# Four moves in one decoder block: a sum of squares two pumps later, two inverses on another DMA queue, a recurrence one pump later, a last norm one pump sooner

## The chip, the core and the metric

The kernel runs on one core of a Trainium2 chip. A core has five engines that work side by side, each with its own instruction stream: TensorE (PE in the profile; PEld is its weight load), VectorE (DVE), ScalarE (ACT), GpSimd (POOL) and SyncE (SP), which here only issues DMAs. DMAs can be issued from the streams of SP, ACT and GpSimd; an issue stands in order with that engine's other work. The metric is the time of one execution on the device in microseconds (us); lower is better. Several runs of the kernel are given with their median, and one more execution was recorded by the profiler.

## The reference

One decoder block on x of 512 tokens by 2048, in fp32. An adaLN vector c gives shifts, scales and gates; two token mixers run side by side on the normed input; a SwiGLU channel mixer follows, and a last RMSNorm.

```python
mod = c_act @ w_ada[l] + b_ada[l]
sh_a, sc_a, gt_a, sh_f, sc_f, gt_f = ...
h = _rmsnorm(x, norm_mix[l]) * (1.0 + sc_a) + sh_a
p = h @ w_in[l]
c_q, c_kv, k_pe, q_g, k_g, v_g, z, b_logit, a_logit, gate_logits = _split_cols(p)
y_a = _mla_branch(c_q, c_kv, k_pe, ...) @ w_o_mla[l]
y_b = _gdn_branch(qkv, z, b_logit, a_logit, ...) @ w_o_gdn[l]
g_a, g_b = jnp.split(jax.nn.sigmoid(gate_logits), 2, axis=-1)
x = x + gt_a * ((g_a * y_a + g_b * y_b) @ w_o[l])
h = _rmsnorm(x, norm_ffn[l]) * (1.0 + sc_f) + sh_f
gate, up = jnp.split(h @ w_gate_up[l], 2, axis=-1)
x = x + gt_f * ((jax.nn.silu(gate) * up) @ w_down[l])
return _rmsnorm(x, final_norm)
```

Two parts of it matter here. The first `_rmsnorm(x, ...)` needs the sum of squares of every token over 2048 channels. The gated DeltaNet branch (`_gdn_branch`) works on 8 heads in chunks of 64 tokens, and for every chunk and head it solves with a unit lower triangular 64 by 64 matrix:

```python
Lmat = jnp.where(strict, jnp.einsum('bhncd,bhnsd->bhncs', kb, k) * decay, 0.0)
A = Lmat + jnp.eye(CHUNK)
sol = lax.linalg.triangular_solve(A, rhs, left_side=True, lower=True, unit_diagonal=True)
```

The kernel inverts these triangles instead: 32 by 32 diagonal blocks first, by forward substitution on VectorE, then the off-diagonal blocks of 32 and of 64 by small products on TensorE.

## The kernel before

**Products and weights.** An fp32 product is made of three products of halves. Each weight tile of 128 by 1024 is loaded (`raw`), rounded into `hi` on ACT (L263), and the rest goes into `lo` on VectorE (L264); activations have such halves too (`hh`, `hl`). A weight unit, two k-tiles, is 24 matmuls on TensorE: hh by hi, hl by hi, hh by lo. There are five raw slots (`RAWS`) and four pairs of hi and lo (`SPLITS`). All matmuls, and all DMAs of `load` (on SP's queue) and `side` (on GpSimd's queue), carry line 155, that of a helper; so they are told apart by their tiles.

**Chains and pumps.** The main line is a list of units. Everything else (statistics, the DeltaNet groups, norms) is written as Python generators, called chains. The driver (L49 to L127) counts the matmuls of the main line and after every 12 (`GROUP`) it "pumps": each chain runs up to its next `yield`. `yield n` lets n pumps go by. So a number behind a `yield` says how many times 12 matmuls stand on TensorE between two steps of a chain. Where the main line needs a result, it runs the chain to its end at once (`drv.finish`). The order on SP, GpSimd and TensorE is the program's order; that on VectorE and ACT is set by a planner when the kernel is built, with the program's data dependencies kept. All engines then run their streams in order.

**The sum of squares.** `x_statistics` (L460) adds the squares of the 16 channel tiles on VectorE (`x_sum`, L456), then TensorE sums over the partitions in eight small instructions (`xss`, four matmuls in the code), VectorE takes the reciprocal root (L396, L229 to L233) and puts it on a diagonal (`diag`, L472), and a product with ones spreads it to all partitions (`rbc`, copied to `r_all` on ACT, L476). The main line, which is then multiplying `ga` products, needs `r_all` where the fully normed input is first used: `start_h` (L1499) calls `drv.finish(chains["stat"])` there. On VectorE the sums of `rawm` run beside this: `rawm` tiles are those of w_ada, 192 loads of 512 KB on SP's queue that take the same raw slots, and each is multiplied and summed in one operation (L435).

**The DeltaNet groups.** `gdn(g)` is one chain for each of two groups of heads. Forward substitution on VectorE (L797, L799) fills `fsX`; it is written to DRAM (`fso`, two DMAs, L803) and read back in another layout (`T32`, four DMAs, L807; the profile calls it T). Fourteen pumps later come T's transpose (L815), the products `M1` (profile: M) with copies on ACT (L825) and VectorE (L826), three pumps later `X1` (profile: X) with negated copies into `T64` (L847, ACT) and `T64T` (L848, VectorE), then `M2` with copies on ACT (L867), three pumps later `X2` with negated copies (L878), and then the recurrence over chunks (`py`, `pks`, `po`). Beside it on ACT run the copies of the conv inputs (`cp`, L523) and of the conv's first tap (L510), on VectorE the other taps (`cv`, L513).

**The tail.** `finished` (L2006) is a chain that the last down-projection unit of the first half of the tokens adds: it sums squares on TensorE (`hss`), takes the reciprocal root, spreads it (`hbc`), scales x (L2013) and writes it out in eight DMAs, while the main line multiplies the last `dnt` products of the second half.

Of the kernel before, what the change touches and what calls it, by code (L numbers as in the profile page):

```python
# [171 lines left out]
def block_kernel(ctx: ExitStack, tc: tile.TileContext, a: dict, out, out_t):  # L172
    nc = Core(tc, PINNED)
# [16 lines left out]
    def S(s, dt=F32):  # L190
        return slots.tile([P, 512], dt, tag="s", name=nm(s))

    def PS(s):
        return psum.tile([P, 512], F32, tag="ps", name=nm(s))
# [4 lines left out]
    def load(dst, src):  # L199
        nc.sync.dma_start(dst, src)  # L200

    def side(dst, src):
        nc.gpsimd.dma_start(dst, src)
# [3 lines left out]
    def tok(j):  # L207
        return slice(j * P, (j + 1) * P)
# [184 lines left out]
    def token_rstd(ss, n, inv):  # L393

        v, y, u = (C(nm("rs"), [P, n]) for _ in range(3))
        nc.vector.tensor_scalar(v[:], ss, inv, EPS, op0=ALU.mult, op1=ALU.add)  # L396
        rsqrt(y[:], v[:], u[:])
        return y
# [50 lines left out]
    def square(k):  # L449

        if k == 0:
            nc.scalar.activation(x_sum[:], xT[k][:], AF.Square)
            return
        s = S("sq")
        tc.keep_in_program_order(nc.scalar.activation(s[:], xT[k][:], AF.Square))
        tc.keep_in_program_order(nc.vector.tensor_tensor(x_sum[:], x_sum[:], s[:], ALU.add))  # L456
# [3 lines left out]
    def x_statistics():  # L460
        for k in range(KT):
            square(k)
            if k % 2:
                yield
        yield 2
        ps = PS("xss")
        for t in range(NT):
            mm(ps[:, t:t + 1], x_sum[:, tok(t)], ones[:, 0:1], start=True, stop=True)
        x_rstd = token_rstd(ps[:, 0:NT], NT, 1.0 / D)
        diag = S("diag")  # L470
        for t in range(NT):
            nc.vector.tensor_scalar(diag[:, tok(t)], ident, x_rstd[:, t:t + 1], None, op0=ALU.mult)  # L472
        yield 5
        ps = PS("rbc")
        mm(ps[:], ones[:], diag[:], start=True, stop=True)
        nc.scalar.copy(r_all[:], ps[:])  # L476
# [85 lines left out]
    def head():  # L562
# [39 lines left out]
        for k in range(KT):  # L602
# [9 lines left out]
            u.post()  # L612
        drv.deep = AHEAD
        chains["stat"] = drv.add(x_statistics())

    wide = S("wide", F32R)
# [80 lines left out]
    fso = [dram.tile([4, NT, 4, 32, 32], F32, name=f"fso{g}") for g in range(2)]  # L697

    def gdn(g):
# [89 lines left out]
        fsX = fsX_[:].rearrange("p (i a) -> p i a", a=16)  # L789
# [10 lines left out]
            if j % 4 == 3:  # L800
                yield
        for hf in range(2):
            nc.scalar.dma_start(fso[g].rearrange("b c h i a -> (b c h) i a")[:, :, 16 * hf:16 * hf + 16], fsX[64 * hf:64 * hf + 64])  # L803
        del fsX_, fsX, fsT, fsL
        T32 = S("T32")
        for b in range(4):
            nc.scalar.dma_start(T32[32 * b:32 * b + 32, :].rearrange("p (n a) -> p n a", a=32),  # L807
                                fso[g][b].rearrange("c h i a -> i (c h) a"))
        yield 14
        T64 = [S("T64"), S("T64")]  # L810
# [48 lines left out]
        for hf in range(2):  # L859
# [6 lines left out]
            m2 = S("M2")  # L866
            nc.scalar.copy(m2[64:128, :], p3[64:128, :])  # L867
            M2.append(m2)
        yield 3
        for hf in range(2):  # L870
            p4 = PS("X2")
            for c in (2 * hf, 2 * hf + 1):
# [427 lines left out]
    def view(tile_, seg):  # L1300

        return tile_[:].rearrange("p (k n) -> p k n", k=2)[:, :, seg[1]:seg[1] + seg[2]]
# [11 lines left out]
    def part_rstd(segs):  # L1314

        ps = PS("hss")
        n = sum(seg[2] for seg in segs) // P
        todo = []
        for i in range(max(len(sums[seg]) for seg in segs)):
            t0 = 0  # L1320
            for seg in segs:
                if i < len(sums[seg]):
                    v = view(sums[seg][i], seg)
                    todo += [(t0 + t, v[:, j, tok(t)]) for t in range(seg[2] // P) for j in range(2)]
                t0 += seg[2] // P
        for i, (t, v) in enumerate(todo):
            mm(ps[:, t:t + 1], v, ones[:, 0:1], start=i == 0, stop=i == len(todo) - 1, skip_group_check=True)
        for seg in segs:
            del sums[seg]
        y = token_rstd(ps[:, 0:n], n, 1.0 / D)  # L1330
        diag = S("diag")
        for t in range(n):
            nc.vector.tensor_scalar(diag[:, tok(t)], ident, y[:, t:t + 1], None, op0=ALU.mult)
        return diag, n * P

    def spread(diag, n):
        ps = PS("hbc")
        mm(ps[:, 0:n], ones[:], diag[:, 0:n], start=True, stop=True)
        return ps[:, 0:n]
# [153 lines left out]
    def mixing():  # L1493
# [25 lines left out]
        def start_a():  # L1519
            ch["A"] = drv.add(gdn(0))  # L1520
# [6 lines left out]
        def start_b():  # L1527
            ch["B"] = drv.add(gdn(1))
# [316 lines left out]
    def ffn():  # L1845
# [126 lines left out]
        def last_unit(segs, fs):  # L1972
# [15 lines left out]
            def post():  # L1988
                for i, f in enumerate(fs):
                    o = 0  # L1990
                    for h, c0, m in segs:
                        add_gated(h, f, box["ps"][i][:, o:o + m], gt_ffn, c0)
                        o += m
                q = fs[0] // 2
                for seg in segs:
                    squares(q, seg, nc.gpsimd if q < 7 else nc.vector)
                for h, c0, m in segs:
                    for k in fs:
                        v = half_of(x2[h][q], k)[:, c0:c0 + m]
                        nc.scalar.activation(v, v, AF.Copy, scale=n_out[:, k:k + 1])  # L2000
                if q == 7:
                    drv.add(finished(segs))
# [1 line left out]
            return Unit(mms=mms, pre=pre, post=post)  # L2004

        def finished(segs):  # L2006
            yield 2
            diag = part_rstd(segs)
            yield 2
            r = spread(*diag)  # L2010
            for q in range(8):
                v = view(x2[0][q], segs[0])
                nc.vector.tensor_tensor(v, v, r.unsqueeze(1).broadcast_to([P, 2, 256]), ALU.mult)  # L2013
                load(out[256 * q:256 * q + 256, :].rearrange("(k p) n -> p k n", p=P), v)
                if q % 2:
                    yield
# [89 lines left out]
```

## Time and profile before

| | us |
|---|---|
| three runs | 2811.27, 2808.55, 2806.51 |
| their median | 2808.55 |
| profiled execution | 2811.78 |
| its span | 2810.0 |
| TensorE busy | 2777.4 (99% of the span) |
| VectorE busy | 1876.6 (67%) |
| ACT busy | 1040.1 (37%) |
| GpSimd busy | 175.2 (6%) |

The span runs from the first to the last instruction; 1.8 us of the profiled execution lie around it. The mean granted clock of TensorE was 0.995 of full speed. In the rows of the profile, a line such as `138.62 1.86 PE L155 MATMUL xss<-ones,x_sum ... x8 [4.97 <-DVE x_sum L456]` gives the start, the duration, the engine, the line of the kernel, the operation, output and inputs, shape and count; the bracket gives the idle time of that engine before it and what ended it. "ACTq" is the issue side of ACT, where its DMAs are issued. A windows row gives the length of a stretch, then the busy time and count of each engine, the granted clock, the busy share of the DMA engines, and GB/s.

### The profile page before, as it was taken

To read this page: it belongs to the slowest core of one execution; us is meant where nothing else is said; L and a number is where in the kernel's file an instruction comes from. 1 tells how busy PE (TensorE), PEld (TensorE's weight loads), DVE (VectorE), ACT (ScalarE), POOL (GpSimd) and SP (SyncE) were. 2 spreads that over 40 slices of the span, in tenths; PEclk is the share of its full clock that TensorE was granted. 3 is DMA by queue.
4 is the path that set the end of the run, shared out by engine and by line. 5 is a ranking of instruction groups with operands and counts; after the bars stand their busy time and mean duration, and the time that the engine had idled before them with its cause. 6 is when DMAs were issued, how large, how long until landed. Compare 5 with 4: busy or idle time off the path is not lost.

```text
span 2810.0 us, 43334 instructions
## 1 busy us (share of the span) xinstructions
PE 2777.4 (99%) x16944; PEld 2473.5 (88%) x16944; DVE 1876.6 (67%) x3172; ACT 1040.1 (37%) x1433; POOL 175.2 (6%) x250
## 2 busy tenths in 40 slices
PE   9999999999999999999999999999999999999997
PEld 7788788788888888888999999999999998888887
DVE  8884666666868547774587888888888873223235
ACT  3443432442344343222374444444444442112123
POOL 0000011001000000001000000000000040030001
PEclk9999999999999999999999999999999999999999
DMA  9995555545646549885453443344344475363241
GB/s 352 320 374 172 159 174 176 173 134 166 190 131 192 191 142 327 286 292 170 160 175 96 137 136 125 129 136 136 124 132 136 136 260 174 113 206 123 98 135 61
DMA packets 307014, 495.22 MB, mean 176 GB/s; under 512 B 47380, under 2 KB 160180, under 8 KB 306680
## 3 DMA queue, kind: packets, MB, share of 16 engines
q1 hardware_dynamic: 260232, 417.03, 45.7%
q0 software_dynamic: 14304, 46.45, 4.6%
q10 hardware_dynamic: 32272, 28.97, 3.1%
q8 instruction: 132, 2.16, 0.3%
q14 instruction: 74, 0.61, 0.1%
HBM read 440.97 MB, written 51.40 MB: 175 GB/s over the span
## 4 chain that ended last, share of the span: by engine, by line
PE 93%; DVE 3%; DMA 2%; issue 1%; ACT 1%; ACTq 0%; SPq 0%; DVEq 0%; POOL 0%; POOLq 0%
PE m L155 29%; PE dn L155 15%; PE wo L155 6%; PE gb L155 5%; PE v L155 4%; PE gu L155 3%; PE z L155 3%; PE ya L155 3%; PE yb L155 3%; PE s L155 3%; PE k L155 2%; PE ga L155 2%; PE qk L155 2%; PE ckv L155 2%; PE q L155 2%; PE cq L155 1%
## 5 line engine op out<-in xcount | busy, mean ns | idle before, releaser
L264 DVE TENSOR_TENSOR lo<-raw,hi 128x1024 fp32r<-128x1024 f32 x338 | 413.8, 1227 | 452.7 <-ACT hi L263 443.6
L263 ACT CAST hi<-raw 128x1024 fp32r<-128x1024 f32 (+1 forms) x338 | 352.4, 1044 | 938.9 <-PE dn L155 255.3
L435 DVE CUSTOM_DVE_ANT_0 rawm<-rawm,cbc 128x1024 f32<-128x1024 f32 x192 | 232.9, 1225 | 150.0 <-DMA rawm<-in_w_mod_dram 149.9
L1720 ACT CAST hi<-sums 128x1024 fp32r<-128x1024 f32 x160 | 167.8, 1049 | 325.9 <-PE m L155 234.2
L155 PE MATMUL m<-h2h,lo 128*128 128x256 f32 x960 | 271.7, 283 | 0.0
L155 PE MATMUL m<-h2l,hi 128*128 128x256 f32 x960 | 271.7, 283 | 0.0
L155 PE MATMUL m<-h2h,hi 128*128 128x256 f32 x960 | 271.7, 283 | 0.0
L1721 DVE TENSOR_TENSOR lo<-sums,hi 128x1024 fp32r<-128x1024 f32 x160 | 195.8, 1224 | 109.7 <-ACT hi L1720 109.6
L155 PE MATMUL dn<-ah,hi 128*128 128x512 f32 x640 | 249.1, 389 | 0.0
L155 PE MATMUL dn<-al,hi 128*128 128x512 f32 x640 | 249.0, 389 | 0.0
L155 PE MATMUL dn<-ah,lo 128*128 128x512 f32 x640 | 249.0, 389 | 0.0
L155 PEld LDWEIGHTS m<-h2h,hi 128*128 128x128 f32 x960 | 184.3, 192 | 0.0
L155 PEld LDWEIGHTS m<-h2l,hi 128*128 128x128 f32 x960 | 184.3, 192 | 0.0
L155 PEld LDWEIGHTS m<-h2h,lo 128*128 128x128 f32 x960 | 184.3, 192 | 0.0
L1720 ACT CAST hi<-raws 128x768 fp32r<-128x768 f32 x160 | 133.5, 834 | 118.0 <-PE m L155 88.8
L1721 DVE TENSOR_TENSOR lo<-raws,hi 128x768 fp32r<-128x768 f32 x160 | 152.1, 951 | 3.4 <-ACT hi L1720 3.4
L155 PEld LDWEIGHTS dn<-ah,hi 128*128 128x128 f32 x640 | 120.1, 188 | 25.4 <-DVE g L1737 0.3
L155 PEld LDWEIGHTS dn<-ah,lo 128*128 128x128 f32 x640 | 120.1, 188 | 24.9
L155 PEld LDWEIGHTS dn<-al,hi 128*128 128x128 f32 x640 | 120.1, 188 | 24.8
L1712 DVE TENSOR_TENSOR sums<-sums,raws 128x256 f32<-128x256 f32 x320 | 134.3, 420 | 4.2
L1712 DVE TENSOR_TENSOR sums<-raws 128x512 f32<-128x512 f32 x160 | 109.9, 687 | 8.8 <-DMA raws<-in_w_gate_up_dram 6.1
L155 PE MATMUL wo<-mh,hi 128*128 128x512 f32 (+1 forms) x320 | 111.2, 347 | 0.0
(498 smaller groups left out, 7202.3 us busy)
## 6 DMA issues: line engine op xcount, KB each, us to landing
rawm<-in_w_mod_dram SPq DMA_DIRECT2D x192, 512.0 KB, 5.4
raws<-in_w_gate_up_dram SPq DMA_DIRECT2D x320, 256.0 KB, 3.0
raw<-in_w_in_dram SPq DMA_DIRECT2D x144, 512.0 KB, 4.5
raw<-in_w_down_dram SPq DMA_DIRECT2D x88, 512.0 KB, 3.8
raw<-in_w_o_dram SPq DMA_DIRECT2D x40, 512.0 KB, 3.9
rawa<-in_w_in_dram SPq DMA_DIRECT2D x32, 512.0 KB, 4.3
raw<-in_w_gate_up_dram SPq DMA_DIRECT2D x48, 256.0 KB, 3.0
a_dram<-ah POOLq DMA_DIRECT2D x40, 256.0 KB, 2.4
```

Source lines behind the costliest of these rows:

```text
L155: return self.tc.keep_in_program_order(f(*args, **kwargs))
L263: nc.scalar.copy(hi[:], raw[:])
L264: (lo_eng or nc.vector).tensor_tensor(lo[:], raw[:], hi[:].bitcast(F32), ALU.subtract)
L435: nc.vector.tensor_tensor_reduce(raw, raw, c, 1.0, 0.0, ALU.mult, ALU.add, parts[:, k, half:half + 1])
L1712: add = lambda o, x, y: nc.vector.tensor_tensor(o, x, y, ALU.add)
L1720: nc.scalar.copy(hi[:], src)
L1721: nc.vector.tensor_tensor(lo[:], src, hi[:].bitcast(F32), ALU.subtract)
```

## The change

Four edits, in three chains and one queue:

- `x_statistics`: `yield 2` before the `xss` products becomes `yield 4`. The products stand two pumps (24 matmuls) later.
- `gdn`, L803 and L807: the DMAs that write `fso` and read `T32` are issued with `side`, on GpSimd's queue, where they were issued on ACT's. Twelve DMAs in all, six for each group, with the same sizes and layouts.
- `gdn`, L869: `yield 3` between M2 and X2 becomes `yield 4`. X2 and all that follows in the group stand one pump (12 matmuls) later.
- `finished`: the first `yield 2` becomes `yield`. The sums of squares of the last first-half segment stand one pump sooner, with what follows.

No product, copy or DMA is added or removed. The planner sets the order on VectorE and ACT anew.

```diff
@@ x_statistics
             if k % 2:
                 yield
-        yield 2
+        yield 4
         ps = PS("xss")
@@ gdn
         for hf in range(2):
-            nc.scalar.dma_start(fso[g].rearrange("b c h i a -> (b c h) i a")[:, :, 16 * hf:16 * hf + 16], fsX[64 * hf:64 * hf + 64])
+            side(fso[g].rearrange("b c h i a -> (b c h) i a")[:, :, 16 * hf:16 * hf + 16], fsX[64 * hf:64 * hf + 64])
         del fsX_, fsX, fsT, fsL
         T32 = S("T32")
         for b in range(4):
-            nc.scalar.dma_start(T32[32 * b:32 * b + 32, :].rearrange("p (n a) -> p n a", a=32),
+            side(T32[32 * b:32 * b + 32, :].rearrange("p (n a) -> p n a", a=32),
                                 fso[g][b].rearrange("c h i a -> i (c h) a"))
         yield 14
@@ gdn
             M2.append(m2)
-        yield 3
+        yield 4
         for hf in range(2):
             p4 = PS("X2")
@@ finished
         def finished(segs):
-            yield 2
+            yield
             diag = part_rstd(segs)
```

## The prediction

> **What bounds the kernel now.** I read the busy times first. TensorE has 1% of the span left, so an edit is worth what it does to TensorE's stalls, to its clock, or to the ends of the span.
>
> ```profile
> PE 2777.4 (99%) x16944; PEld 2473.5 (88%) x16944; DVE 1876.6 (67%) x3172; ACT 1040.1 (37%) x1433; POOL 175.2 (6%) x250
> ```
>
> The waits of TensorE come next. Each happened once; the third is the start of the kernel, and what is not shown is below 1 us.
>
> ```profile
> PE xss L155 <- DVE x_sum L456: 5.0, 1, 5.0
> PE k L155 <- DVE lo L264: 3.7, 1, 3.7
> PE cb L155 <- DMA crow<-in_c_dram: 3.1, 1, 3.1
> PE X L155 <- issue: 1.7, 1, 1.7
> ```
>
> The windows view shows that the other three each cost more than the wait. Its columns are length, busy time of PE, PEld, DVE, ACT and POOL, then TensorE's granted clock, the DMA share and GB/s.
>
> ```profile
> 137.55:144.38 6.83, 5.76 (x18) 4.89 (x19) 5.97 (x14) 1.58 (x2) 0.00 (x0) 0.50 0.87 293
> 144.38:153.00 8.62, 8.62 (x40) 7.12 (x39) 7.68 (x20) 2.87 (x5) 0.60 (x2) 1.00 0.92 313
> 516.43:523.26 6.83, 5.12 (x12) 4.06 (x13) 6.78 (x11) 4.29 (x9) 0.00 (x0) 0.50 0.55 172
> 560.80:567.63 6.83, 6.83 (x28) 5.65 (x29) 6.34 (x12) 1.88 (x3) 0.00 (x0) 0.50 0.31 97
> ```
>
> Around each wait lies a stretch of 6.83 us at half clock. Busy TensorE in it does half the work, so half its busy time is lost: 2.88, 2.56 and 3.41 us. With the waits, the three places cost 7.85 us (xss), 6.25 us (k) and 5.11 us (X). The four edits touch these three and the tail. [...]
>
> The unit of all shifts is the price of one matmul, from a row of the chain of waits:
>
> ```profile
> 154.24 43.53 PE ga L155 x192
> ```
>
> 43.53 / 192 = 0.227 us; a pump (12 matmuls) is 2.72 us, a unit (24) 5.44 us.
>
> **A: the xss products two pumps later (L465).** It adds and removes nothing. The eight products move behind 24 further ga matmuls; rbc does not move, because the start of the next stage forces the chain to its end there.
>
> ```profile
> 133.26 0.39 PE L155 MATMUL ga<-hh,lo 128*128 128x512 f32 x1
> 138.62 1.86 PE L155 MATMUL xss<-ones,x_sum 128*128 128x1 f32 x8 [4.97 <-DVE x_sum L456]
> 137.88 0.68 DVE L456 TENSOR_TENSOR x_sum<-x_sum,sq 128x512 f32<-128x512 f32 x1
> 140.52 0.16 DVE L396 TENSOR_SCALAR rs<-xss 128x4 f32<-128x4 f32 x1 [0.81 <-PE xss L155]
> 140.60 1.23 DVE L264 TENSOR_TENSOR lo<-raw,hi 128x1024 fp32r<-128x1024 f32 x1
> 151.90 0.92 DVE L472 TENSOR_SCALAR diag<-kc,rs 128x128 f32<-128x128 f32 x4
> 152.69 1.22 DVE L435 CUSTOM_DVE_ANT_0 rawm<-rawm,cbc 128x1024 f32<-128x1024 f32 x1
> L155 PE MATMUL rbc<-diag,ones x2: 590/590/591, 153.2 to 153.7; 128*128 128x512 f32 x2
> 138.50:152.80 14.30, 14.18 (x55) 11.85 (x56) 12.50 (x32) 3.34 (x5) 0.54 (x1) 0.79 0.91 307
> ```
>
> Today TensorE gets to xss at about 133.5 and waits for x_sum until 138.6. With 24 matmuls more it gets there at 133.5 + 5.44 = 138.9, after x_sum is done: the wait of 4.97 goes, and the half clock with it. But the next thing is late. From xss to rbc VectorE needs 14.3 us and is busy for 12.5 of them; it runs the rsqrt steps between the sums of rawm and the lo halves, in an order fixed ahead. TensorE has 24 matmuls instead of 48 between xss (about 1 us at full clock) and rbc, so it is at rbc at 138.9 + 1 + 5.4 = 145.3 and waits for diag, some 8.6 us. What counts is when rbc can run. VectorE's order changes in two places: the lo of 140.60 now stands ahead of L396 (that moves the chain by about half a microsecond, which later idle time absorbs), and the rawm sum of 152.69 (1.22 us) now stands ahead of diag. That makes diag about 1.1 us later: rbc at 154.3 instead of 153.2. After a stall this long TensorE restarts at half clock; now it is at full clock there. By the two restarts above (2.88, 2.56) I take 2.6. A = +1.1 + 2.6 = **+3.7 us**. Ends: +1.4 (diag 0.3 early, half of half a stretch, 1.7) and +4.8 (1.4 late, half of 6.83). The lo halves are too far ahead of TensorE afterwards to hide any of it elsewhere, so it goes into the end.
>
> **B: the inverses' way through DRAM on GpSimd's queue (L803, L807).** Two writes of 128 KB and four reads of 64 KB per group leave ACT's queue, where each stands in order with ACT's work.
>
> ```profile
> 496.47 3.98 ACTq L803 DMA_DIRECT2D fso<-fsX  x2
> 500.54 1.06 ACT L263 CAST hi<-raw 128x1024 fp32r<-128x1024 f32 x1 [12.88 <-DMA fso<-fsX]
> 503.68 2.50 ACTq L807 DMA_DIRECT2D T<-fso  x4
> 506.22 2.06 ACT L523 COPY cp<-q 128x512 f32<-128x512 f32 x4 [4.62 <-issue]
> 500.64 1.23 DVE L435 CUSTOM_DVE_ANT_0 rawm<-rawm,cbc 128x1024 f32<-128x1024 f32 x1 [4.25 <-DMA rawm<-in_w_mod_dram]
> 508.93 8.02 DVE L513 SCALAR_TENSOR_TENSOR cv<-cp,columns,cv 128x511 f32<-128x511 f32 x12 [5.92 <-ACT cv L510]
> 516.86 3.49 DVE L264 TENSOR_TENSOR lo<-raw,hi 128x1024 fp32r<-128x1024 f32 x3
> 518.14 0.80 PE L155 MATMUL k<-hh,lo 128*128 128x512 f32 x1 [3.69 <-DVE lo L264]
> 525.72 1.20 PE L155 MATMUL M<-T,LT 32*32 32x32 f32 x64
> 547.56 2.07 PE L155 MATMUL M<-T,LT 64*64 64x64 f32 x32
> ```
>
> ACT sits in these issues until 506.2; hi and the four cp copies queue behind them, cv on VectorE behind cp, and lo, which TensorE lacks from 518.14 − 3.69 = 514.4 on, behind cv. Without the issues cp runs from about 497, cv on VectorE waits only for the rawm sum (501.9), and the lo is ready at 501.9 + 8.0 + 1.2 = 511.1, 3.3 us early. The wait and the half clock of group 0 go: **−6.3**. In group 1 the waits view has no such wait, so the same move gives 0.
>
> GpSimd now issues them, and nothing shows these shapes on its queue. The nearest rows are its own copy with the most elements, its reloads of 256 KB, and ACT's landing and issue times for the writes (ns, min/median/max):
>
> ```profile
> L155 POOL DMA_DIRECT2D g_dram<-gt_ffn x1 | 1.2, 1169 | 0.0
> L155 POOL DMA_DIRECT2D al<-a_dram x40 | 28.7, 716 | 3.2 <-DMA ah<-a_dram 1.4 <-PE m L155 0.7 <-DMA al<-a_dram 0.6
> fso<-fsX ACTq DMA_DIRECT2D x4, 128.0 KB, 6.1
> L803 ACTq DMA_DIRECT2D fso<-fsX x4: 552/1942/3372, 496.5 to 746.7; - x4
> ```
>
> fsX is done at 496.4. Short end: two writes at 1.17, landing 6.1, four reads at 0.72, landing 6.1 again: T32 at 513.8. Long end: writes at ACT's longest, 3.37 each, reads at 1.17: 520.0. I take 513.8, since its issues are GpSimd's own. M1, the first product that needs T32, would come at 525.72 − 6.3 = 519.4, so it does not wait. On GpSimd only the memsets of T64 stand behind these DMAs, and they are wanted after T32.
>
> But T32 now also heads a line on VectorE. Its transpose comes ahead of a lo whose raw slot the next rawm load takes, and from there each rawm load takes the slot of the sum before it: seven sums in a row, where before two loads could be under way. Such a step (sum, load, landing, sum) was already seen on VectorE, three steps from the first of these rows to the last:
>
> ```profile
> 539.74 1.23 DVE L435 CUSTOM_DVE_ANT_0 rawm<-rawm,cbc 128x1024 f32<-128x1024 f32 x1 [2.29 <-DMA rawm<-in_w_mod_dram]
> 554.72 1.22 DVE L435 CUSTOM_DVE_ANT_0 rawm<-rawm,cbc 128x1024 f32<-128x1024 f32 x1 [1.08 <-DMA rawm<-in_w_mod_dram]
> ```
>
> (554.72 − 539.74) / 3 = 5.0 us. With the transpose at 513.8 and the lo done at 516.2, the sums start at about 520.3, 525.3, 530.3, 535.3, 540.3, 545.3 and 550.3. Three things hang on them. M1's copy comes behind the second (1.2) and a lo (1.2): 528.4, while X1, three pumps behind M1, is due at 519.4 + 1.2 + 8.2 = 528.8. M2's last operand comes behind the fifth, 541.5 and two copies of 0.4: 542.4, and M2's second half is due at 547.56 − 6.3 + 1.0 = 542.2: a wait of 0.2. The third is part C. B = **−6.1 us**. Ends: −6.3, and −0.4 (long end of T32: a wait of 0.6 at M1, a restart of 2.6, 2.7 at M2).
>
> [...]
>
> **C: X2 one pump later (L869).** Nothing is added; everything behind it in the group moves 12 matmuls.
>
> ```profile
> 557.95 1.14 PE L155 MATMUL X<-T64T,M 64*64 64x64 f32 x16
> 560.79 1.93 PE L155 MATMUL X<-T64T,M 64*64 64x64 f32 x16 [1.70 <-issue]
> 560.11 0.58 ACT L867 COPY M<-M 64x512 f32<-64x512 f32 x1
> ```
>
> The second half of X2 waits for M2's second copy on ACT, done at 560.69; the copy itself stands behind cv work of VectorE, which stands behind the seventh sum. With B and C the second half is due at 557.95 + 1.14 + 2.72 − 6.1 = 555.7. The copy comes after the seventh sum (551.5), three cv steps (8.02 / 12 each, 2.0), a lo (1.2), and on ACT an activation and the copy (0.6 each): 555.9, and with gaps between them 556.6. So a wait of 0.9 stays of 1.70, and the half clock (3.41) goes: **−4.2 us**. Ends: −5.1; and 0, if the copy is 2 us or more late and the clock drops as before. In group 1 X did not wait: 0. The recurrence behind X2, one pump later under other products, I cost at 0.
>
> **D: hss one pump sooner (L2007).** The tail is bound by VectorE:
>
> ```profile
> 2778.36 0.95 PE L155 MATMUL hss<-ones,sq 128*128 128x1 f32 x8
> 2784.00:2801.00 17.00, 11.34 (x51) 9.05 (x49) 16.07 (x38) 5.50 (x14) 0.00 (x0) 0.97 0.28 100
> ```
>
> hss at 2775.6 lets the rsqrt and the scalings of x move into idle time before 2784; but 16.07 of the last 17 us are busy, so at most 17 − 16.07 = 0.9 can be won, and the order may give nothing. **−0.6**, ends −1.0 and 0.
>
> Sum: 3.7 − 6.1 − 4.2 − 0.6 = −7.2. The profiled execution took 2811.78 us (span 2810.0), 3.2 above the median of the runs, 2808.55; so it would be 2804.6, and against the median **2801.3 us**.
>
> **Rivals.**
> - *A is clean.* If diag were ready when TensorE gets to rbc, A would give its whole 7.85: −18.8 in all, 2789.8 us. For it: x_sum is no longer awaited. Against it: VectorE's 12.5 busy of 14.3 us, which TensorE cannot shorten. 0.07.
> - *The line of sums is late*, the steps being 5.4 us instead of 5.0, or T32 2 us later: some 3 us of waits at M2 and X2 and one restart at half clock (X2's cost 3.41). 3.7 − 11.4 + 3 + 3.4 − 0.6 = −1.9: C does little of what it says, 2806.6 us. For it: B takes TensorE 6 us closer to a line that does not get shorter. [...] 0.36.
> - *T32 is late (slower).* One mechanism: GpSimd issues these small-run DMAs much slower than ACT did, and TensorE waits at M1. Without B the sum is at most 3.7 − 5.1 − 0.6 = −2.0; each microsecond of T32 after 519.4 costs one, and 2.6 come on top for the restart. At 525 that is 5.6 + 2.6 − 6.3, B about +2, no change in all; from 530.7 on the kernel is over 5.6 us slower. At 533 it gives about 2816.5 us. For it: each write has many short runs, and no row of this queue has them. Against it: it takes 34 us where ACT took about 13. 0.19.
>
> **How the numbers follow.** My forecast has 0.38. A measurement of this kernel tells 0.2% (5.6 us) from no change. The forecast and the clean A are faster, 0.45; the late line is the same, 0.36; late T32 is slower, 0.19. All lower ends add up to 1.4 − 6.3 − 5.1 − 1.0 = −11.0 (2797.6), all upper ends to 4.8 − 0.4 + 0 + 0 = +4.4 (2812.9). The range, 2796.5 to 2812.5, leaves out the clean A and most of late T32; the forecast's own is 2797.6 to 2803.
>
> **What would show it.** A: no wait at xss, one of 7 to 10 us at rbc, half clock after 154. B: no wait at k near 514, ACT's cp at about 497, the transpose of T32 between 512 and 516, sums of rawm behind it 5 us apart. C: X2's second half with less than 1 us of wait, full clock behind it. D: hss 2.7 us earlier against the end of the products before it. The prediction falls if rbc does not wait, if T32 lands after 520, or if the clock is halved at M2 or X2.

## The result, and the profile after

The changed kernel took 2812.5 us (median of 17 runs, 2808.78 to 2817.53) against 2808.55 us before (17 runs on the same chip, 2806.0 to 2814.23). The ratio is 1.0016, with a 95% interval of 1.0009 to 1.0024: slower, by a little less than the 0.2% that the chances were set by. The forecast was 2801.3 and faster. One run of `d_only`, a kernel of the experiments, took 5497.0 us at a granted clock of 0.472, and its ratio leaves that run out.

First the busy row of the page, and TensorE's waits of at least 1 us that are not at the start of the kernel:

```profile
PE 2775.1 (99%) x16944; PEld 2471.4 (88%) x16944; DVE 1882.1 (67%) x3172; ACT 1039.4 (37%) x1433; POOL 183.6 (7%) x262
```

```profile
PE rbc L155 <- DVE diag L472: 8.8, 1, 8.8
PE X L155 <- issue: 3.6, 1, 3.6
...
PE cT L155 <- DVE M L826: 1.5, 1, 1.5
```

The waits at xss and at k are gone, as the change means them to be. In their place stand one at rbc, a doubled one at X2 and a new one at cT in group 1. TensorE did the same products and was busy for 2.3 us less; it stood idle for longer.

To place the microseconds, I took the start of one and the same matmul of the main line in both traces, at points where no chain is half done, and subtracted. The table gives how late each kernel is against the kernel before at these points; a step in a row is what the stretch between two points cost or gained. The names of the others are explained below.

| kernel | 133 | 160 | 380 | 500 | 530 | 545 | 640 | 760 | 900 | 2200 | 2700 | end |
|---|---|---|---|---|---|---|---|---|---|---|---|---|
| changed | +1.5 | +4.5 | +4.5 | +3.5 | −2.8 | −2.8 | +0.1 | +0.1 | +1.8 | +1.8 | +3.0 | +3.0 |
| a_only | +1.3 | +4.7 | +4.7 | +3.8 | +2.8 | +3.1 | +2.6 | +2.6 | +2.7 | +2.6 | +3.9 | +3.9 |
| b_only | +1.2 | +1.3 | +1.3 | +0.9 | −5.4 | −5.4 | +1.4 | +1.4 | +1.4 | +1.4 | +1.6 | +1.6 |
| c_only | +2.9 | +4.2 | +4.2 | +4.0 | +4.3 | +4.3 | −0.4 | −0.4 | −0.4 | −0.4 | 0.0 | 0.0 |
| d_only | +1.9 | +2.5 | +2.5 | +5.7 | +6.2 | +6.3 | +4.0 | +4.0 | +4.1 | +4.1 | +4.5 | +4.5 |
| bc4 | +1.4 | +1.5 | +1.5 | +0.6 | −5.8 | −5.8 | −2.6 | −2.6 | −0.2 | −0.2 | +3.1 | +3.1 |
| b_no8 | +1.7 | +2.2 | +2.2 | +2.2 | −4.2 | −4.2 | −9.2 | −9.2 | −9.2 | −9.2 | −7.7 | −7.7 |
| bc6 | −0.4 | +0.4 | +0.4 | +0.4 | −6.0 | −6.0 | −6.6 | −6.6 | +0.2 | +0.5 | +1.3 | +1.3 |
| b0c6 | −0.3 | −0.4 | −0.4 | −0.6 | −6.9 | −6.9 | −7.8 | −7.8 | −7.8 | −7.8 | −7.5 | −7.5 |
| b0c5 | +2.3 | +3.2 | +3.2 | +3.2 | −3.1 | −3.1 | +0.4 | +0.4 | +1.0 | +1.0 | +0.8 | +0.8 |
| x_split | +2.8 | −2.9 | −1.2 | −1.5 | −2.2 | −2.1 | −2.6 | −2.6 | −2.6 | −2.6 | −2.2 | −2.2 |
| b0c6x | +5.2 | −1.8 | −1.3 | −1.5 | −7.9 | −7.9 | −12.3 | −12.2 | −12.1 | −12.2 | −12.3 | −12.3 |

A caution on how to read it: each row is one execution, and "end" is the last matmul, some 15 us ahead of the end of the span. Before 133 the rows differ by some 3 us without an edit there (only the last two have one), most of it from products near 12 us that wait for the first activations; between 2200 and 2700 by up to 3.3. In the stretches between, rows without an edit there move too: by up to 1.3 from 133 to 160 (`c_only`), by 3.2 from 380 to 500 and by some −2 from 545 to 640 (both `d_only`), by −1.0 from 500 to 530 (`a_only`). The profiled execution of the kernel before happens to be early at the start. So the steps in the stretches of the edits are read, not the last column.

For the changed kernel they are: A (133 to 160) +3.0, B at k (500 to 530) −6.3, X2 and the recurrence (545 to 640) +2.9, group 1 (760 to 900) +1.7, the tail (2700 to the end) 0.0.

**Where A went.** TensorE's timeline, then VectorE's, then a window just behind rbc:

```profile
140.39 1.04 PE L155 MATMUL xss<-ones,x_sum 128*128 128x1 f32 x8
...
155.79 2.08 PE L155 MATMUL rbc<-diag,ones 128*128 128x512 f32 x2 [8.79 <-DVE diag L472]
```

```profile
153.72 1.22 DVE L435 CUSTOM_DVE_ANT_0 rawm<-rawm,cbc 128x1024 f32<-128x1024 f32 x1
...
154.86 0.87 DVE L472 TENSOR_SCALAR diag<-kc,rs 128x128 f32<-128x128 f32 x4
```

```profile
155.79:159.50 3.71, 3.71 (x7) 2.29 (x8) 3.44 (x7) 0.78 (x2) 0.00 (x0) 0.50 1.02 402
```

xss no longer waits. rbc comes at 155.79 instead of 153.22; with the 1.5 us that this execution was late already, that is 1.1 later. The sum of rawm ahead of diag is there. Then 3.71 us run at half clock.

**Where B's and C's gain went.** The queue of ACT is free as forecast, and GpSimd is not slow. ACT, GpSimd and VectorE of the changed kernel:

```profile
496.56 2.04 ACT L523 COPY cp<-q 128x512 f32<-128x512 f32 x4
```

```profile
501.56 2.19 POOL L155 DMA_DIRECT2D fso<-fsX  x2 [43.61 <-issue]
509.72 2.61 POOL L155 DMA_DIRECT2D T<-fso  x4 [5.96 <-issue]
```

```profile
500.84 0.18 DVE L799 TENSOR_TENSOR fsX<-fsX,fsT 128x16 f32<-128x16 f32 x1
...
505.06 8.02 DVE L513 SCALAR_TENSOR_TENSOR cv<-cp,columns,cv 128x511 f32<-128x511 f32 x12
...
515.25 0.71 DVE L815 STREAM_TRANSPOSE T32T<-T 128x512 f32<-128x512 f32 x1
...
526.59 1.23 DVE L435 CUSTOM_DVE_ANT_0 rawm<-rawm,cbc 128x1024 f32<-128x1024 f32 x1 [2.19 <-DMA rawm<-in_w_mod_dram]
...
531.19 1.23 DVE L435 CUSTOM_DVE_ANT_0 rawm<-rawm,cbc 128x1024 f32<-128x1024 f32 x1 [1.49 <-DMA rawm<-in_w_mod_dram]
...
537.18 1.23 DVE L435 CUSTOM_DVE_ANT_0 rawm<-rawm,cbc 128x1024 f32<-128x1024 f32 x1 [3.62 <-DMA rawm<-in_w_mod_dram]
...
542.15 1.22 DVE L435 CUSTOM_DVE_ANT_0 rawm<-rawm,cbc 128x1024 f32<-128x1024 f32 x1 [2.43 <-DMA rawm<-in_w_mod_dram]
...
544.04 1.23 DVE L264 TENSOR_TENSOR lo<-raw,hi 128x1024 fp32r<-128x1024 f32 x1
...
550.03 1.23 DVE L435 CUSTOM_DVE_ANT_0 rawm<-rawm,cbc 128x1024 f32<-128x1024 f32 x1 [4.32 <-DMA rawm<-in_w_mod_dram]
...
556.75 1.23 DVE L435 CUSTOM_DVE_ANT_0 rawm<-rawm,cbc 128x1024 f32<-128x1024 f32 x1 [2.12 <-DMA rawm<-in_w_mod_dram]
```

The line of sums is there, each waiting for its load. From 526.59 to 542.15 its steps are 4.6, 6.0 and 5.0 us, where 5.0 was forecast; the last two are 7.9 and 6.7. SP's queue shows why:

```profile
543.41 0.37 SPq L155 DMA_DIRECT2D raw<-in_w_in_dram  x1
545.29 0.34 SPq L155 DMA_DIRECT2D rawm<-in_w_mod_dram  x1
551.29 0.37 SPq L155 DMA_DIRECT2D raw<-in_w_in_dram  x1
552.43 0.34 SPq L155 DMA_DIRECT2D rawm<-in_w_mod_dram  x1
```

The slot of the sum that ended at 543.4 goes to a `raw` load; the next `rawm` load is behind it in the queue and goes out at 545.29, when the lo of 544.04 frees a slot. At 551.29 and 552.43 the same happens again. So the step is longer by the way to the next lo. The last sum ends at 558.0, and M2's second copy and X2 follow from it:

```profile
561.97 0.58 ACT L867 COPY M<-M 64x512 f32<-64x512 f32 x1
```

```profile
557.87 1.14 PE L155 MATMUL X<-T64T,M 64*64 64x64 f32 x16
562.65 1.94 PE L155 MATMUL X<-T64T,M 64*64 64x64 f32 x16 [3.63 <-issue]
```

The copy ends at 562.55, TensorE was there at 557.87 + 1.14 = 559.0, and from 562.65 to 569.40 the clock was about half:

```profile
562.65:569.40 6.75, 6.75 (x28) 5.62 (x29) 5.16 (x9) 1.26 (x2) 0.00 (x0) 0.52 0.62 189
```

**Group 1.** M1's copy on VectorE again, in the kernel before:

```profile
763.88 0.70 DVE L815 STREAM_TRANSPOSE T32T<-T 128x512 f32<-128x512 f32 x1
...
769.40 1.67 DVE L978 TENSOR_SCALAR ckv<-ckv,rs 128x512 f32<-128x512 f32 x4
771.10 0.70 DVE L826 COPY M<-M 32x512 f32<-32x512 f32 x1
```

In the changed kernel, with the product that waits for it:

```profile
767.73 1.67 DVE L978 TENSOR_SCALAR ckv<-ckv,rs 128x512 f32<-128x512 f32 x4
769.31 0.70 DVE L815 STREAM_TRANSPOSE T32T<-T 128x512 f32<-128x512 f32 x1
...
775.47 0.70 DVE L826 COPY M<-M 32x512 f32<-32x512 f32 x1
```

```profile
776.22 0.66 PE L155 MATMUL cT<-kc,ckv 128*128 128x128 f32 x4 [1.50 <-DVE M L826]
```

VectorE's new order puts the transpose behind the scaling of ckv. That is only a part of the delay. The copy starts 25.1 us after the group's last `fsX` in the kernel before (746.0 to 771.1) and 26.5 after it now (748.9 to 775.5), 1.4 more. The last `fsX` itself comes 2.9 later, while TensorE is where it was (+0.1 at 760). `c_only`, with these DMAs on ACT, has such a late `fsX` too (748.1), and its copy ends at 774.00, 0.05 us ahead of cT. Why `fsX` comes later was not followed.

### The profile page after: what moved, and what is told of

Same layout as the page of the kernel before. It is cut to its first block, busy times and chain, and to the rows that moved or that the text cites. A ratio compares the mean times of both kernels' runs of the same rounds, so it can differ in the third digit from the quotient of the medians.

```text
span 2813.0 us, 43322 instructions
## 1 busy us (share of the span) xinstructions
PE 2775.1 (99%) x16944; PEld 2471.4 (88%) x16944; DVE 1882.1 (67%) x3172; ACT 1039.4 (37%) x1433; POOL 183.6 (7%) x262
## 4 chain that ended last, share of the span: by engine, by line
PE 71%; DVE 1%; DMA 1%; issue 0%; ACT 0%; DVEq 0%; ACTq 0%
PE m L155 28%; PE dn L155 15%; PE wo L155 6%; PE gu L155 3%; PE ya L155 3%; PE yb L155 3%; PE gb L155 3%; PE qk L155 2%; PE sc L155 1%; PE z L155 1%; PE dnl L155 1%; PE v L155 1%; PE yT L155 1%; PE qpe L155 0%; PE pT L155 0%
## 5 line engine op out<-in xcount | busy, mean ns | idle before, releaser
L155 PEld LDWEIGHTS dn<-ah,lo 128*128 128x128 f32 x640 | 120.2, 188 | 25.1
```

Of the source, the lines that this page charges most:

```text
L155: return self.tc.keep_in_program_order(f(*args, **kwargs))
```

## The experiments

**One edit at a time.** Theory 1 was read from the two traces; each rival stands with its kernel. `a_only` has the first hunk of the diff, `b_only` the second, and so on.

> Only the xss products two pumps later. Theory 1 (read from the two traces): the wait of 5.0 us at xss is replaced by one of 8 to 9 us at rbc for diag, rbc runs 1 to 2 us later than in the kernel before, and the half clock moves behind rbc: 2.5 to 4 us slower. Rival: the loss of the changed kernel sits elsewhere (start of the kernel, the GpSimd queue); then this edit alone is within 1 us of the kernel before.

Measured: 2814.03 us against 2809.77 for the kernel before, ratio 1.0012 (1.0002 to 1.0021). rbc waits 8.7 us:

```profile
PE rbc L155 <- DVE diag L472: 8.7, 1, 8.7
```

The stretch from 133 to 160 costs +3.4 in this trace, +3.0 in that of the changed kernel, and between −0.1 and 1.3 in the kernels with xss and its sum as they were. In the trace theory 1 holds and the rival falls; by the times alone the loss could be as small as 0.6 us (0.0002 of 2809.77).

> Only the DMAs of fso and T32 on GpSimd's queue. Theory 1: the wait at k (3.7 us and half clock, 6.3 in all) goes, but M2's second copy does not come earlier, so X2's second half waits 5 to 7 us instead of 1.7, and in group 1 cT waits about 1.5 us for M1's copy: within 2 us of the kernel before. Rival (the recorded sum for B): 6 us faster, with X2's wait below 3 us and no wait in group 1.

Measured: 2811.66 us, ratio 1.0004 (0.9995 to 1.0013). The wait at k is gone (500 to 530: −6.3), and both halves of X2 now wait:

```profile
555.70 1.94 PE L155 MATMUL X<-T64T,M 64*64 64x64 f32 x16 [3.10 <-issue]
562.14 1.94 PE L155 MATMUL X<-T64T,M 64*64 64x64 f32 x16 [4.51 <-issue]
```

The stretch from 545 to 640 costs +6.8: B by itself pays back all that it won. In group 1 there was no wait at cT; that part of theory 1 was wrong for this kernel, whose TensorE comes to group 1 later by 1.3 us (+1.4 at 760 against +0.1).

> Only X2 one pump later. Theory 1: with the wait at k still there, M2's second copy comes at the same time as before and X2's second half 2.7 us later, so its wait of 1.7 us and the half clock behind it go: 4 to 5 us faster. Rival: the copy or a later step of the recurrence moves along, and a wait stays at X2 or comes at po: within 1.5 us of the kernel before.

Measured: 2807.43 us, ratio 0.9993 (0.9984 to 1.0002), which does not tell it from no change. In the trace X2 runs in one piece, the clock stays full (a product of v takes 0.39 us ahead of X2 and 0.39 or 0.40 from 567.29 on), and the stretch from 545 to 640 gains 4.7:

```profile
564.94 2.07 PE L155 MATMUL X<-T64T,M 64*64 64x64 f32 x32
```

C does what it was forecast to do as long as B is not there. A part of the 4.7 belongs to the kernel before, which lost 5.1 us at X2, 1.7 by the wait and 3.41 by 6.83 us at half clock: `a_only`, `d_only` and `x_split`, with X2 where it was, gain 0.5, 2.3 and 0.5 us in this stretch without an edit there. They wait 2.8, 1.1 and 2.8 us at X2, so by an estimate (5.1 less the gain and the wait) the half clock cost them 1.7 to 1.8 us where it cost 3.41.

> Only the hss products one pump sooner. Theory 1: VectorE is the bound of the tail and its last steps come at the same time: within 0.3 us in the profile, no change in the times. Rival (the recorded sum for D): 0.6 us faster.

Measured: 2810.5 us (median of the ten runs that the ratio counts), ratio 1.0001 (0.9992 to 1.001). hss does come 2.7 us sooner, as forecast: in the changed kernel, which is 3.0 late there, at 2778.62, in the kernel before at 2778.36. But from 2700 to the last matmul the lag does not change, here or in any kernel with D, and from there to the end of the span it changes by 0.0 us in the changed kernel and +0.3 here. So the forecast's −0.6 was not seen in the traces; the times, uncertain by some 2.5 us, could not show it.

**Is it the line of sums?** In `b_no8`, B alone, eight loads and their sums are left out, among them the two sums that come late:

```diff
             for k in range(KT):
                 box = {}
+                if chunk == 2 and 8 <= k < 12:
+                    yield Unit()
+                    yield Unit(None, (lambda k=k: done(slice(k - 3, k + 1))) if k % 4 == 3 else None)
+                    continue
                 for half in range(2):
```

> B alone, with eight of the w_ada loads and their sums left out (chunk 2, k 8 to 11, so a quarter of one shift is not computed): the two sums of rawm that stand between X1's copies and M2's copies are gone, everything else in that stretch stays. Theory 1 (M2's copies on ACT hang on the serial line of rawm sums on VectorE): the waits at X2, 3.1 and 4.5 us in B alone, fall below 1 us together. Rival (they hang on ACT's hi copies or on GpSimd's DMAs): they stay above 4 us together.

Measured, in one execution: X2 in one piece at 553.77 without a wait, M2's copies before it:

```profile
549.37 0.59 ACT L867 COPY M<-M 64x512 f32<-64x512 f32 x1
...
553.69 0.58 ACT L867 COPY M<-M 64x512 f32<-64x512 f32 x1
```

```profile
553.77 2.08 PE L155 MATMUL X<-T64T,M 64*64 64x64 f32 x32
```

In `b_only` the copies stand at 555.02 and 561.47. ACT's hi work and GpSimd's DMAs are the same in both kernels, the loads and sums are not: M2's copies hang on them. (Its time, 2804.23 us, has less work in it.)

**Both gains at once?** `bc4` has B and C as in the changed kernel, without A and D. `bc6` has B and `yield 6` in place of 4; `b0c6` and `b0c5` have B in group 0 alone and `yield 6` or 5 there.

```diff
-            nc.scalar.dma_start(fso[g]...
+            (nc.scalar.dma_start if g else side)(fso[g]...
...
-        yield 3
+        yield (3 if g else 6)
```

> The changed kernel without A and D: B and X2 one pump later. Theory 1: no wait at k, X2's second half waits 2 to 4 us and halves the clock, cT in group 1 waits 1 to 3 us: within 3 us of the kernel before, and 3 to 4 us less than the changed kernel, which A accounts for. Rival (A costs nothing once B and C are there): as slow as the changed kernel, 3 to 5 us over the kernel before.

Measured: 2811.18 us against 2810.73, ratio 1.0005 (0.9997 to 1.0014).

```profile
PE X L155 <- issue: 5.1, 1, 5.1
...
PE cT L155 <- DVE M L826: 2.2, 1, 2.2
```

X2 waits even more than the 2 to 4 us expected. With B and C in place but no A, the kernel is level with the kernel before; the two ratios, 1.0005 here and 1.0016 for the changed kernel, put A (with D) at about 3 us, but their intervals overlap.

> B with three pumps more ahead of X2 (yield 6) in both groups, without A and D. Theory 1: M2's second copy ends near 562.5 and X2's second half comes 5.4 us later than in the changed kernel: no wait at k, none at X2, full clock: 9 to 11 us less than the kernel before, if nothing else in group 1 turns up. Rival (the copy moves with TensorE): X2 still waits 2 to 4 us and the time is within 4 us of the kernel before.

Measured: 2806.22 us against 2809.81, ratio 0.9988 (0.9979 to 0.9997): a third of what theory 1 said. X2 waits no more, but waits come up behind it (2.1 us at py), and in group 1 cT waits, and the stretch from 760 to 900 costs +6.8, 2.3 more than the wait:

```profile
PE cT L155 <- DVE M L826: 4.5, 1, 4.5
```

> The same for group 0 alone; in group 1 the DMAs stay on ACT and the yield stays 3. Theory 1: as B with yield 6, and no wait at cT in group 1: 9 to 11 us faster. If the wait of 1.5 us at cT in the changed kernel comes from the DMAs on GpSimd in group 1, this kernel is 1 to 2 us faster than the one with both groups; if not, the two are the same.

Measured: 2805.2 us, ratio 0.9988 (0.9978 to 0.9997). cT does not wait, and group 1 costs 0.0; in the times of the two kernels that makes no difference that can be told. It does not show that the wait at cT comes from the DMAs of group 1 on GpSimd: of the 5.9 us by which M1's copy starts earlier here than in `bc6` (765.9 against 771.8), 3.5 are there at the last `fsX` already (740.8 against 744.3), ahead of these DMAs. Among the kernels that have them on GpSimd, the wait goes with TensorE's lag at 760: 0 in `b_only` (+1.4), 1.5 us in the changed kernel (+0.1), 2.2 in `bc4` (−2.6), 4.5 in `bc6` (−6.6). As at X2, the copy moves less than TensorE does: it starts at 773.95 in the first of these four and at 771.76 in the last. `b_no8`, at −9.2 but with eight loads fewer, has no wait. The stretch from 545 to 640 gives only −0.9, since the recurrence now waits instead:

```profile
PE py L155 <- DVE r L890: 2.0, 1, 2.0
...
PE pS L155 <- ACT yd L907: 1.2, 1, 1.2
```

> B and X2 two pumps later (yield 5), in group 0 only. M2's second copy ends near 560 to 561 in the runs of B; X2's second half is due about 2.7 us earlier than with yield 6. Theory 1: a wait below 1 us at X2, the later waits at pS and py (1.2 and 2.0 us with yield 6) smaller by one pump: 5 to 9 us less than the kernel before, level with yield 6. Rival: X2 waits 2 us or more with half clock, and the kernel is 3 us or more slower than with yield 6.

Measured: 2809.72 us against 2810.73, ratio 0.9995 (0.9986 to 1.0003). The rival was nearer: X2 waits 1.7 us and py behind it 3.0.

**Less work on VectorE.** `x_split` gives the adds for odd k to GpSimd, into a second sum that xss adds up in PSUM:

```diff
+        if k % 2:
+            nc.gpsimd.tensor_tensor(x_sum2[:], x_sum2[:], s[:], ALU.add)
+            return
         tc.keep_in_program_order(nc.vector.tensor_tensor(x_sum[:], x_sum[:], s[:], ALU.add))
...
-            mm(ps[:, t:t + 1], x_sum[:, tok(t)], ones[:, 0:1], start=True, stop=True)
+            mm(ps[:, t:t + 1], x_sum[:, tok(t)], ones[:, 0:1], start=True, stop=False)
+            mm(ps[:, t:t + 1], x_sum2[:, tok(t)], ones[:, 0:1], start=False, stop=True)
```

> The kernel before, with half of the adds of squares (odd k) on GpSimd into a second sum, and eight more small products at xss. Theory 1 (xss and rbc both wait for VectorE's line, so only less work on it helps): the wait of 5.0 us at xss falls by 3 us or more, and rbc gets no wait: 3 to 8 us faster. Rival (x_sum is late because of the loads of x or of ACT's squares): the wait stays at 4 to 5 us, no change.

Measured: 2808.02 us against 2809.81, ratio 0.9994 (0.9985 to 1.0003), not told from no change. In the trace the waits move as theory 1 said, and rbc does not wait:

```profile
PE ga L155 <- DVE lo L264: 4.1, 4, 1.4
...
PE xss L155 <- DVE x_sum L459: 1.0, 1, 1.0
```

The stretch from 133 to 160 gains 5.7. But 2.8 are lost before 133, the lag going from 0.0 at 120 to 2.8 at 130: TensorE waits for lo, and on VectorE a lo beside an add of GpSimd took 2.30 us (at 122.05), the next one, with no add beside it, 1.21 (at 129.95); more of this below.

> B and yield 6 in group 0, and half of the adds of squares on GpSimd. If the two places are independent, the gains add: 2 us less than with B and yield 6 alone, 7 to 11 us less than the kernel before. Rival: VectorE, earlier at the start, only waits for loads later, and the sum is no better than B and yield 6 alone.

Measured: 2799.35 us (five runs) against 2810.73, ratio 0.9959 (0.9947 to 0.9972). This is the best of all, faster than both kernels, and by more than the parts (0.9988 and 0.9994, together 0.9982). In the trace its stretch at X2 gives −4.4 where `b0c6` has −0.9: the waits at pS and py are down to 0.4 us or less. Why they are was not tried.

## Why the prediction was wrong

- **A: right, and a little too large.** Forecast +3.7: no wait at xss, 8.6 us at rbc, diag 1.1 later, a restart of 2.6. Measured 8.8 us, 1.1 later, and 1.9 for the restart (3.0 − 1.1; 3.71 us at half clock lose 1.86).
- **B at k: right.** −6.3 forecast and measured in every kernel with B (500 to 530: −6.3 to −6.4). cp, cv and lo came as worked out; T32's transpose was due 513.8 − 496.4 = 17.4 us after fsX and came within 515.25 − 501.0 = 14.2: the reads landed 2.4 us after their issue, where the prediction took the writes' 6.1.
- **The issues on GpSimd: not slow.** The two writes took 2.19 us to issue and the four reads 2.61, with VectorE's lo and cv at work beside them; the short end had taken 2.34 and 2.88.
- **C together with B: wrong; this is the step that failed.** The prediction put the wait that stays at X2 at 0.9 us and the half clock at none: −4.2. It was 3.6 us with the half clock. TensorE came when it was due: 559.0, less the 3.5 us that this execution was late at 500, is 555.5, and 555.7 was forecast. M2's second copy did not: its end at 562.55, less the same 3.5, is 559.0, and 556.6 was forecast. The mechanism, the line of sums, had been seen; the length of its last two steps failed, 7.9 and 6.7 us where 5.0 each was taken. "From there each rawm load takes the slot of the sum before it" does not hold for these two: the slot goes to a raw load, and the rawm load behind it waits for the next lo. These 4.6 us show as only 2.4 at the copy because, by luck, the line had begun earlier than forecast: the sum forecast for 540.3 came at 542.15, less 3.5 is 538.6. With B and C together the stretch from 545 to 640 cost +2.9, where −4.0 was forecast (0.2 at M2, −4.2 at X2): 6.9 of the 7.2 us that the whole change was to gain. Of that, 0.7 is a wait at `po`, in the recurrence that the prediction had at 0. The nearest rival is "the line of sums is late", at 0.36; its price was smaller.
- **Group 1: wrong.** "The same move gives 0" was an argument from a view of waits alone, which cannot show how near M1's copy already stood to cT: 2.6 us (771.8 to 774.4). Now the copy ends 1.5 us behind TensorE, and the stretch costs 1.7.
- **D: −0.6 forecast, 0.0 measured,** within its ends.

With the measured terms the sum of A, B, X2, group 1 and D is 3.0 − 6.3 + 2.9 + 1.7 + 0.0 = +1.3, while the medians differ by +3.95, at least 2.5 by the interval (0.0009 of 2808.55). So C with B takes the gain away, and the sign turns with group 1 and with a remainder that is not settled. Between the two profiled executions, 2.95 us apart, the rest lies where nothing was edited: +1.5 before 133, −1.0 from 380 to 500, +1.2 from 2200 to 2700. They can't decide it: at cT alone the wait was between 0 and 4.5 us in the five kernels with B in both groups, with 6.8 us lost in that stretch in one of them.

## What to carry to other kernels

A wait that ends on an engine is worth its length only if the next thing that TensorE needs comes earlier too: follow that operand back to what paces it, here a line of loads, sums and slots that no edit touched, and count who takes which slot. Bringing TensorE forward makes the next late operand dearer: B gains 6.3 us at k and alone loses 6.8 again at X2, and C, which alone gains 4.7 there, still left a loss of 2.9 behind B. Where a forced point follows, as rbc does here, moving a product back only moves the wait; taking work off the engine that is late (and checking that no neighbour is slowed by it) removed it in the trace of `x_split`, whose time alone can't be told from no change.

## What the runs showed of the hardware

In `b0c6x` and `x_split`, between 118 and 136 us, VectorE's operations with two inputs that start while GpSimd adds two tensors took about 1.1 us longer each; the one exception is a lo of `b0c6x` that starts 0.01 us into an add. From `b0c6x`, two sums and two adds in one stretch:

```profile
126.71 1.77 DVE L459 TENSOR_TENSOR x_sum<-x_sum,sq 128x512 f32<-128x512 f32 x1
128.40 2.30 DVE L435 CUSTOM_DVE_ANT_0 rawm<-rawm,cbc 128x1024 f32<-128x1024 f32 x1
...
131.78 0.68 DVE L459 TENSOR_TENSOR x_sum<-x_sum,sq 128x512 f32<-128x512 f32 x1
132.38 1.21 DVE L435 CUSTOM_DVE_ANT_0 rawm<-rawm,cbc 128x1024 f32<-128x1024 f32 x1
```

```profile
125.86 3.77 POOL L155 TENSOR_TENSOR x_sum<-x_sum,sq 128x512 f32<-128x512 f32 x2 [0.16 <-ACT sq L455]
132.61 2.12 POOL L155 TENSOR_TENSOR x_sum<-x_sum,sq 128x512 f32<-128x512 f32 x1 [2.98 <-ACT sq L455]
```

The two operations that start while GpSimd's adds run (125.86 to 129.63) take 1.77 and 2.30, the same ones a little later 0.68 and 1.21. The last of these meets an add too, but started ahead of it (132.38 against 132.61).

Behind a stall of 1.7 us at X2 the clock was 0.50 for 6.83 us (kernel before). Behind another of 1.7 us there (`b0c5`) products of v started 0.43 us apart for 3.0 us (564.84 to 567.83), then 0.23 apart again from 568.17 on; behind one of 1.1 us (`d_only`) the estimate above leaves 1.7 us lost to the half clock. At cT the stretch from 760 to 900 cost 1.7 us with a stall of 1.5 (changed kernel), 2.4 with one of 2.2 (`bc4`) and 6.8 with one of 4.5 (`bc6`): 0.2 more than the stall twice, then 2.3. The window around the first of these:

```profile
574.00:800.00 226.00, 222.53 (x1317) 186.44 (x1317) 166.43 (x361) 85.58 (x144) 25.88 (x33) 1.00 0.55 165
```

The granted clock (the column behind POOL) is 1.00. X2's products are small ones of 64x64; what decides how the clock goes behind a short stall was not settled.
